# Score blocks of a linear recurrence in a compact tile, masked once for all row groups

## The chip, the cores and the metric

One Trainium2 chip, of which the kernel uses 1 core. The metric is the device time of one execution in microseconds (us), the median of several runs. A core has five engines with a queue of instructions each: TensorE (PE) multiplies matrices, VectorE (DVE) and ScalarE (ACT) work on elements, GpSimd (POOL) does small work, and SyncE (SP) starts transfers. An engine runs its queue in order and waits at an instruction until its operands are there.

## The reference

A decoder trunk of two layers over 256 tokens of width 2048. Each layer projects the normed input with `w_in`, runs sliding-window attention on one half of the heads and a gated linear recurrence (HGRN2) on the other, projects both with `w_out`, and then has a feed-forward block. The change touches the recurrence and the scaling of attention's outputs:

```python
f = lbf + (1.0 - lbf) * jax.nn.sigmoid(z)
k_in = (1.0 - lbf) * jax.nn.sigmoid(-z)
...
b = jnp.cumsum(g_, axis=2)                       # g = log f
decay = jnp.exp(where(causal, b_t - b_s, MASK))  # per channel
a = jnp.einsum('bhtk,bhsk,bhtsk->bhts', q_, k_, decay)
o = jnp.einsum('bhts,bhsv->bhtv', a, v_) + (q_ * exp(b)) @ state
...
o = rms_norm(o, hgrn_gain)
attn = rms_norm(sliding_window_attention(q, k, v, sinks), attn_gain)
```

`a` is a lower triangle of scores whose decay differs from channel to channel.

## The kernel before

Matrix products with weights are made from high and low halves: a weight chunk (`wr`, 128x1024, fetched by SP) is cast by ACT into `wh` (L310), DVE subtracts to get `wl` (L320), and PE makes three products for each tile, xh·wh, xl·wh and xh·wl (L335, L336, L338), twelve matmuls 128x512 a chunk. The input's halves are `ck`.

In a layer, `w_in` is walked in strips of 512 columns: attention's k and v, two strips of q, and then for each of two groups of four recurrence heads the strips f, q, i and g. A group is an object of class `Rec`, whose work runs beside the matmuls of the next strips:

- `done_f` makes f and k with sigmoids and scales f by the bound `lb` (ACT, L951); `done_q` makes q and the pair operand `qd`.
- `levels` computes the triangle of scores by doubling. First PE computes blocks of 32 tokens from `k` and `qd` (`pd`). `up(1)` and `prepare(2)` scale q, k and f for the next step on DVE. Then `four(2, 8)` and `four(8)` (scores L1024, from `qf` of L1010 and L1012) each join four blocks of 2 and of 8 tokens inside the blocks of 32, `up_four` (L1049 to L1059) scales for what comes next, and the loop over 32 and 64 (scores L1097, copies L1101) joins blocks outside them. `up(32)` is the second use of L993.
- The blocks of 32 lie on the diagonal of the 128x128 score tile `at`. They come from PSUM with masks: a product with the identity (L1075), predicated copies with `m_one` (L1077) and three with `m_four` a step (L1039). As the place in `at` differs for each of the four groups of 32 rows, each of them has its own set of instructions, on 32 partitions.
- `out` multiplies `at` with the values `hv` (L1129), `done_i` makes `hv` (L1120), and `px` is the block between both halves of the tokens. The result goes through a transposing store and load (`turn`, `nat`) to `split_shuffled`, which scales with a gain and splits into halves.

A scheduler sets the order of each engine's instructions: it goes by the program's order, in which `yield` and `later(n, ...)` put steps of the recurrence behind parts of the strips, and by `behind(...)`, which puts a step after a named matmul. POOL builds the masks at the start.

Of the kernel before, what the change touches and what calls it, by code (L numbers as in the profile page):

```python
# [8 lines left out]
F32 = mybir.dt.float32  # L9
# [38 lines left out]
def decoder(ctx: ExitStack, tc: tile.TileContext, x, p, positions, w_in, attn_sinks,  # L48
# [126 lines left out]
    def gain_cols(base, l, n):  # L175
        return gT[:, base + l * n: base + (l + 1) * n]
# [99 lines left out]

        return a.rearrange("p k (a j) -> p k a j", a=4)

    def split_shuffled(d, gcols, hl, t, wide=False):
        d, = d  # L280
        h, lo = (quarters(a[:, :, t * P:(t + 1) * P]) for a in hl)
        if gcols is None:
            split(d, h, lo)
            return
        for b in range(4):
            g = gcols[:, b:b + 1]
            if wide:
                S.activation(d[:, b], d[:, b], AF.Copy, scale=g)
            else:
                S.activation(h[:, b], d[:, b], AF.Copy, scale=g)  # L290
                V.scalar_tensor_tensor(lo[:, b], d[:, b], g, h[:, b].bitcast(F32),
                                       op0=ALU.mult, op1=ALU.subtract)
        if wide:
            split(d, h, lo)

    def new_ck():
        return [xp.tile([P, 4, SEQ], F32R, tag="ck", name="ck", bufs=14) for i in range(2)]
# [297 lines left out]
    m_up = cp.tile([P, P], F32, name="m_up")  # L595
    m_prev = cp.tile([P, P], F32, name="m_prev")
    m_neg = cp.tile([P, P], F32, name="m_neg")
    m_one = cp.tile([P, 64], F32, name="m_one")
    m_four = cp.tile([P, 2, 192], F32, name="m_four")
    lb = cp.tile([P, DEPTH, 8], F32, name="lb")  # L600
    omlb = cp.tile([P, DEPTH, 8], F32, name="omlb")
    sink = cp.tile([P, DEPTH, 16], F32, name="sink")
# [5 lines left out]
    def constants():  # L608
# [9 lines left out]
        select(m_prev, ones, [[1, P]], -1, -1)  # L618
        G.memset(m_neg, 0.0)
        select(m_neg, m_neg, [[-1, P]], 0, 1, fill=NEG)  # L620
        select(m_one, ones[:, :64], [[-2, 64]], 0, 1)
        select(m_one, m_one, [[2, 64]], 0, -1)
        for si, k in enumerate((2, 8)):
            m = m_four[:, si].rearrange("p (b six k) -> p b six k", six=6, k=k)
            for v0, n in ((0, 3), (3, 2), (5, 1)):
                for base, sign in ((0, 1), (k - 1, -1)):
                    select(m[:, :, v0:v0 + n], ones[:, :32 * n] if sign > 0 else m[:, :, v0:v0 + n],
                           [[-4 * k * sign, 32 // k], [-k * sign, n], [0, k]], base, sign)

        lmax = tiny(8)  # L630
        V.tensor_copy(lmax, lbl[:, 0])
# [123 lines left out]
    for l in range(DEPTH):  # L755
# [56 lines left out]
        def attend(half, t, o):  # L812
            d = shuffled(o, ready=True)
            for _ in range(6):
                yield
            S.copy(quarters(qT[half][:, :, t * P:(t + 1) * P]), d[0])
            yield
            yield from head_pair(half, t)
            if half == 1:
                yield  # L820
                r = sum_rstd(ssa[t], 1024, f"ra{t}")
                d = []
                for h in range(2):
                    b = nat()
                    V.tensor_scalar(turn_order(b), ao[t][:, h].rearrange("p (k q i) -> p k q i", k=4, q=4),
                                    r[:, 0:1], None, op0=ALU.mult)
                    d.append(b)
                for _ in range(18 + 4 * t):
                    yield
                d = [shuffled(b, ready=True) for b in d]  # L830
                for h in range(2):
                    for _ in range(5 - 4 * h):
                        yield
                    split_shuffled(d[h], gain_cols(96, l, 8)[:, 4 * h:4 * h + 4], attn[h], t,
                                   wide=True)

        def head_pair(half, t):

# [80 lines left out]
        class Rec:  # L919


            def __init__(s, grp):
                s.grp = grp
                s.has_v = set()
                s.f = sp.tile([P, 4, SEQ], F32, tag="A", name="f")
                s.k = sp.tile([P, 4, SEQ], F32, tag="B", name="k")
                s.q = sp.tile([P, 4, SEQ], F32, tag="C", name="q")
                s.at = sp.tile([P, NT, 4, P], F32, tag="at", name="at")
                s.ax = sp.tile([P, 4, P], F32, tag="ax", name="ax")
                G.memset(s.at, 0.0)  # L930

            def diagonal(s, j):

                rows = slice(32 * j, 32 * j + 32)
                return rows, s.at[rows].rearrange("p t h m -> p (t h) m")[:, :, rows]

            def done_f(s, t, ps):
                z = nat()
                S.activation(z, ps, AF.Copy, scale=rx(t)[:, 0:1])


                def turn():
                    pt = bank((P, 4, P))
                    for b in range(4):
                        T.transpose(pt[:, b], z[:, b * P:(b + 1) * P], ident)
                    cols = slice(t * P, (t + 1) * P)
                    S.activation(s.f[:, :, cols], pt, AF.Sigmoid)
                    S.activation(s.k[:, :, cols], pt, AF.Sigmoid, scale=-1.0)
                    for h in range(4):
                        c = s.grp * 4 + h  # L950
                        S.activation(s.f[:, h, cols], s.f[:, h, cols], AF.Identity,  # L951
                                     scale=omlb[:, l, c:c + 1], bias=lb[:, l, c:c + 1])
                later(5, turn)

            def done_q(s, t, ps):
# [56 lines left out]
                V.tensor_tensor(qf[:, :, 5], qf[:, :, 4], fv[:, :, 1].to_broadcast([P, n, k]),  # L1012
                                op=ALU.mult)

            def four(s, k, n=None):

                pl = bank((P, NT, 4, 48))
                for t in range(NT):
                    for h in range(4):
                        for j in range(4):  # L1020
                            rows = slice(32 * j, 32 * j + 32)
                            c = h * 64 + t * 32 + 8 * j
                            with behind("pe"):
                                T.matmul(pl[rows, t, h].rearrange("p (b six k) -> p b six k", six=6, k=k),  # L1024
                                         s.k[:, h, t * P + 32 * j:t * P + 32 * j + 32],
                                         s.qf[:, :, c:c + 8].rearrange("p v (b k) -> p b v k", k=k),
                                         start=True, stop=True)
                s.up_four(k)
                if n:
                    s.prepare(n)  # L1030
                for j in range(4):
                    rows, at = s.diagonal(j)
                    at = at.rearrange("p g (b m) -> p g b m", m=4 * k)
                    pv = pl[rows].rearrange("p t h (b m) -> p (t h) b m", m=6 * k)
                    mv = m_four[rows, (2, 8).index(k), 48 * j:48 * j + 48].rearrange(
                        "p (b m) -> p b m", m=6 * k)
                    for v0, n in ((0, 3), (3, 2), (5, 1)):
                        cols = slice(v0 * k, (v0 + n) * k)
                        V.copy_predicated(  # L1039
                            at[:, :, :, (4 - n) * k:4 * k],  # L1040
                            mv[:, :, cols].bitcast(I32).unsqueeze(1)
                            .to_broadcast([32, 8, 8 // k, n * k]),
                            pv[:, :, :, cols])

            def up_four(s, k):
                qv, kv, fv, qf = s.views(k)
# [14 lines left out]
            def levels(s):  # L1061
# [7 lines left out]
                                     s.qd[:, h, t, j], start=True, stop=True)  # L1069
                s.up(1)  # L1070
                s.prepare(2)
                for j in range(4):
                    rows, at = s.diagonal(j)
                    pv = pd[rows].rearrange("p t h m -> p (t h) m")
                    V.tensor_tensor(at, pv[:, :, 0:32], ident[rows, rows].unsqueeze(1)  # L1075
                                    .to_broadcast([32, 8, 32]), op=ALU.mult)
                    V.copy_predicated(  # L1077
                        at.rearrange("p g (b two) -> p g b two", two=2)[:, :, :, 1],
                        m_one[rows, 16 * j:16 * j + 16].bitcast(I32).unsqueeze(1)
                        .to_broadcast([32, 8, 16]), pv[:, :, 32:48])  # L1080
                yield
                yield
                yield
# [2 lines left out]
                yield  # L1086
                yield
                s.four(8)
                yield
                yield  # L1090
                for k in (32, 64):
# [48 lines left out]
            def done_g(s, t, ps):  # L1140
                sg = nat()
                S.activation(sg, ps, AF.Silu, scale=rx(t)[:, 0:1])
                o = s.ot[:, t].rearrange("p h d -> p (h d)")
                V.tensor_tensor(o, o, sg, op=ALU.mult)
                c = 2 + s.grp
                if c not in mix:
                    mix[c] = new_ck()
                gcols = gain_cols(112, l, 8)[:, 4 * s.grp:4 * s.grp + 4]
                if s.grp == 1:
                    later(4, lambda: split_T(blocks4(o), gcols, mix[c], t))  # L1150
                    return
                d = shuffled(o)
                later(6, lambda: split_shuffled(d, gcols, mix[c], t, wide=True))

        if l == 0:
            with tc.issue_after(first.ins):
# [204 lines left out]
```

## Time and profile before

| | |
|---|---|
| median of 3 runs | 2382.85 us (2382.56 to 2384.52) |
| the profiled execution | 2381.94 us |
| its span, first to last instruction | 2380.2 us |
| granted TensorE clock, mean | 0.998 |
| PE busy | 2343.6 us, 98% of the span |
| DVE, ACT, POOL busy | 2012.1, 1424.4, 115.6 us |
| bytes read and written in HBM | 474.57 and 29.36 MB |

The busy time of PE overlaps its weight loads (PEld). A large matmul's duration is modelled and longer than the distance between two starts. Idle time of PE is what the other engines can add to the end. A row of the waits names the waiting line, the awaited one, the sum, the number and the longest. A row of the groups ends with busy us, mean ns of one, and the idle time ahead of them.

### The profile page before, as it was taken

The page shows a single profiled execution, that of the slowest core. Times are in us where ns is not written, and L with a number is a line of the kernel's source. Part 1 is how long each engine was busy: PE and PEld are TensorE (multiplying, and loading weights), DVE is VectorE, ACT ScalarE, POOL GpSimd, SP SyncE. Part 2 cuts the span into 40 slices and gives each one's busy share as a digit, 9 for nine tenths or more (in the row PEclk, how much of TensorE's full clock was granted, in tenths as well). Part 3 has the DMA queues.
Part 4 walks back from the last instruction along what each step waited for, and adds up shares of the span by engine and source line. Part 5 has one row for each costly group of instructions (what it writes and reads, how often), then busy time and mean ns, then how long its engine had stood idle before and what let it go on. Part 6 is the DMA issues. An engine that isn't in the chain of part 4 may idle for free.

```text
span 2380.2 us, 32807 instructions
## 1 busy us (share of the span) xinstructions
PE 2343.6 (98%) x11527; PEld 1928.1 (81%) x11527; DVE 2012.1 (85%) x2587; ACT 1424.4 (60%) x2072; POOL 115.6 (5%) x217
## 2 busy tenths in 40 slices
PE   9999999999999999999999999999999999999999
PEld 7887787887888888888788777878878888888887
DVE  7676987899999899888877769878999989998885
ACT  6565566556556555657656565665666565565564
POOL 4100001000000000001010000010000000000010
PEclk9999999999999999999999999999999999999999
DMA  8656457656566764766776464675765675667753
GB/s 288 217 160 221 160 196 257 219 199 231 190 230 206 254 225 168 259 228 202 240 217 210 140 226 150 224 269 176 236 224 192 207 254 197 230 208 252 243 169 133
DMA packets 301669, 506.11 MB, mean 213 GB/s; under 512 B 23712, under 2 KB 69696, under 8 KB 301504
## 3 DMA queue, kind: packets, MB, share of 16 engines
q1 hardware_dynamic: 301200, 503.93, 63.1%
q8 instruction: 90, 1.47, 0.3%
q14 instruction: 75, 0.61, 0.1%
q10 hardware_dynamic: 240, 0.07, 0.0%
q0 software_dynamic: 64, 0.02, 0.0%
HBM read 474.57 MB, written 29.36 MB: 212 GB/s over the span
## 4 chain that ended last, share of the span: by engine, by line
PE 87%; DVE 9%; issue 1%; ACT 1%; POOL 1%; DMA 1%; SPq 0%; DVEq 0%; ACTq 0%; POOLq 0%
PE acc L338 8%; PE acc L335 8%; PE acc L336 8%; PE accc L426 5%; PE accc L427 5%; PE accc L423 5%; PE acca L427 4%; PE acca L423 4%; PE acce L427 4%; PE acca L426 4%; PE acce L423 4%; PE acce L426 4%; PE accd L427 3%; PE accd L423 3%; PE accd L426 3%; PE ms L423 3%
## 5 line engine op out<-in xcount | busy, mean ns | idle before, releaser
L310 ACT CAST wh<-wr 128x1024 fp32r<-128x1024 f32 x980 | 1005.3, 1052 | 684.4 <-DVE wr L439 212.2
L320 DVE TENSOR_TENSOR wl<-wr,wh 128x1024 fp32r<-128x1024 f32 x980 | 1162.7, 1220 | 213.9 <-ACT wh L310 206.8
L335 PE MATMUL acc<-wh,ck 128*128 128x512 f32 x1056 | 419.9, 398 | 2.3 <-ACT wh L310 1.8
L338 PE MATMUL acc<-wl,ck 128*128 128x512 f32 x1056 | 412.5, 393 | 4.6 <-DVE wl L320 4.5
L336 PE MATMUL acc<-wh,ck 128*128 128x512 f32 x1056 | 414.7, 393 | 0.0
L439 DVE TENSOR_TENSOR wr<-wr 128x1024 f32<-128x1024 f32 (+1 forms) x240 | 244.5, 1044 | 0.9
L338 PEld LDWEIGHTS acc<-wl,ck 128*128 128x128 f32 x1056 | 199.3, 189 | 49.2 <-DVE wl L320 7.4
L335 PEld LDWEIGHTS acc<-wh,ck 128*128 128x128 f32 x1056 | 199.4, 189 | 44.5 <-ACT wh L310 2.6
L336 PEld LDWEIGHTS acc<-wh,ck 128*128 128x128 f32 x1056 | 199.5, 189 | 40.0 <-DVE ck L204 0.5
L423 PE MATMUL acca<-wh,ck 128*128 128x512 f32 x468 | 183.2, 392 | 3.1 <-ACT wh L310 3.1
L427 PE MATMUL acca<-wl,ck 128*128 128x512 f32 x468 | 182.9, 391 | 1.0 <-DVE wl L320 1.0
L423 PE MATMUL acce<-wh,ck 128*128 128x512 f32 x468 | 183.1, 391 | 0.4 <-ACT wh L310 0.4
L427 PE MATMUL acce<-wl,ck 128*128 128x512 f32 x468 | 182.8, 391 | 0.3 <-DVE wl L320 0.3
L426 PE MATMUL acca<-wh,ck 128*128 128x512 f32 x468 | 182.6, 390 | 0.0
L426 PE MATMUL acce<-wh,ck 128*128 128x512 f32 x468 | 182.5, 390 | 0.0
L427 PE MATMUL accd<-wl,ck 128*128 128x512 f32 x368 | 144.9, 394 | 0.0
L423 PE MATMUL accd<-wh,ck 128*128 128x512 f32 x368 | 143.8, 391 | 0.0
L426 PE MATMUL accd<-wh,ck 128*128 128x512 f32 x368 | 143.4, 390 | 0.0
L426 PE MATMUL accc<-wh,ck 128*128 128x512 f32 x368 | 143.4, 390 | 0.0
L427 PE MATMUL accc<-wl,ck 128*128 128x512 f32 x368 | 143.3, 390 | 0.0
L423 PE MATMUL accc<-wh,ck 128*128 128x512 f32 x368 | 143.3, 389 | 0.0
L423 PEld LDWEIGHTS acca<-wh,ck 128*128 128x128 f32 x468 | 88.1, 188 | 22.9 <-ACT wh L310 4.8
(276 smaller groups left out, 3329.4 us busy)
## 6 DMA issues: line engine op xcount, KB each, us to landing
wr<-in_w_in_dram SPq DMA_DIRECT2D x176, 512.0 KB, 5.1
wr<-in_w_ffn_gate_dram SPq DMA_DIRECT2D x176, 512.0 KB, 5.8
wr<-in_w_ffn_up_dram SPq DMA_DIRECT2D x176, 512.0 KB, 6.1
wr<-in_w_ffn_down_dram SPq DMA_DIRECT2D x176, 512.0 KB, 7.2
wr<-in_w_out_dram SPq DMA_DIRECT2D x64, 512.0 KB, 4.9
wr<-in_w_ple_gate_dram SPq DMA_DIRECT2D x64, 512.0 KB, 5.2
turn<-nat SPq DMA_DIRECT2D x86, 256.0 KB, 2.7
nat<-turn SPq DMA_DIRECT2D x344, 64.0 KB, 3.6
```

The lines of the kernel that those rows point to most:

```text
L310: marks["hi"] = S.copy(hi, raw)
L320: marks["lo"] = V.tensor_tensor(lo, raw, hi.bitcast(F32), op=ALU.subtract)
L335: T.matmul(ps[t], xh, hi[:, k], start=first, stop=False)
L336: T.matmul(ps[t], xl, hi[:, k], start=False, stop=False)
L338: marks[t, c] = marks["pe"] = T.matmul(ps[t], xh, lo[:, k], start=False, stop=last)
L423: T.matmul(ps, xh, hi[:, k], start=id(ps) not in opened, stop=False, skip_group_check=True)
L426: T.matmul(ps, xl, hi[:, k], start=False, stop=False, skip_group_check=True)
L427: marks["pe"] = T.matmul(ps, xh, lo[:, k], start=False, stop=k == ks[-1], skip_group_check=True)
L439: V.tensor_tensor(dst, p, q, op=ALU.subtract)
```

## The change

Four parts:

1. The blocks of 32 tokens of all four row groups go to one compact tile `ac` of 128 partitions x 8 x 32, so each mask operation is one instruction over 128 partitions. Four ACT copies then bring them to the diagonal of `at`. The masks are compact (`m_same`, `m_one`, `m_four`), cut on POOL at the start out of the wide ones.
2. `split_shuffled` loses its `wide` form: attention's outputs and those of group 0 are scaled by ACT straight into the high half, with one DVE scalar_tensor_tensor for each quarter, where ACT scaled in place, cast 128x512, and DVE subtracted once.
3. The scaling of `f` moves from ACT to DVE.
4. The planner's order follows from these.

```diff
-    def split_shuffled(d, gcols, hl, t, wide=False):
+    def split_shuffled(d, gcols, hl, t):
...
-            if wide:
-                S.activation(d[:, b], d[:, b], AF.Copy, scale=g)
-            else:
-                S.activation(h[:, b], d[:, b], AF.Copy, scale=g)
-                V.scalar_tensor_tensor(lo[:, b], d[:, b], g, h[:, b].bitcast(F32),
-                                       op0=ALU.mult, op1=ALU.subtract)
-        if wide:
-            split(d, h, lo)
+            S.activation(h[:, b], d[:, b], AF.Copy, scale=g)
+            V.scalar_tensor_tensor(lo[:, b], d[:, b], g, h[:, b].bitcast(F32),
+                                   op0=ALU.mult, op1=ALU.subtract)
...
+        for j in range(4):
+            rows = slice(32 * j, 32 * j + 32)
+            G.tensor_copy(m_same[rows], ident[rows, rows])
+            G.tensor_copy(m_one[rows], one[rows, 16 * j:16 * j + 16])
+            G.tensor_copy(m_four[rows], four[rows, :, 48 * j:48 * j + 48])
...
+                s.ac = sp.tile([P, NT * 4, 32], F32, tag="ac", name="ac")
...
-                        S.activation(s.f[:, h, cols], s.f[:, h, cols], AF.Identity,
-                                     scale=omlb[:, l, c:c + 1], bias=lb[:, l, c:c + 1])
+                        V.tensor_scalar(s.f[:, h, cols], s.f[:, h, cols], omlb[:, l, c:c + 1],
+                                        lb[:, l, c:c + 1], op0=ALU.mult, op1=ALU.add)
...
-                for j in range(4):
-                    rows, at = s.diagonal(j)
...
-                    for v0, n in ((0, 3), (3, 2), (5, 1)):
-                        cols = slice(v0 * k, (v0 + n) * k)
-                        V.copy_predicated(
...
+                at = s.ac.rearrange("p g (b m) -> p g b m", m=4 * k)
...
+                for v0, n in ((0, 3), (3, 2), (5, 1)):
+                    cols = slice(v0 * k, (v0 + n) * k)
+                    V.copy_predicated(
...
+                pv = pd.rearrange("p t h m -> p (t h) m")
+                V.tensor_tensor(s.ac, pv[:, :, 0:32], m_same.unsqueeze(1)
+                                .to_broadcast([P, 8, 32]), op=ALU.mult)
+                V.copy_predicated(
+                    s.ac.rearrange("p g (b two) -> p g b two", two=2)[:, :, :, 1],
+                    m_one.bitcast(I32).unsqueeze(1).to_broadcast([P, 8, 16]), pv[:, :, 32:48])
...
                 s.four(8)
+                for j in range(4):
+                    rows = slice(32 * j, 32 * j + 32)
+                    S.copy(s.at[rows].rearrange("p t h m -> p (t h) m")[:, :, rows], s.ac[rows])
...
-                later(6, lambda: split_shuffled(d, gcols, mix[c], t, wide=True))
+                later(6, lambda: split_shuffled(d, gcols, mix[c], t))
```

DVE's order at the first score block of group 0 in layer 0. L1077, L1075 and L1039 are the masked operations of one row group each; L1049 to L1057 are `up_four`. Before:

```order
L1077 COPY_PREDICATED at<-m_one,ms 32x8x16
L1075 TENSOR_TENSOR at<-ms,ident 32x8x32
L1049 TENSOR_TENSOR q<-q,f 128x128x2
L1077 COPY_PREDICATED at<-m_one,ms 32x8x16
L1075 TENSOR_TENSOR at<-ms,ident 32x8x32
L1050 TENSOR_TENSOR q<-qf,f 128x128x4
L1077 COPY_PREDICATED at<-m_one,ms 32x8x16
L1055 TENSOR_TENSOR k<-k,f 128x256x2
L1039 COPY_PREDICATED at<-m_four,ms 32x8x4x6
L1056 TENSOR_TENSOR f<-f 128x256
L1039 COPY_PREDICATED at<-m_four,ms 32x8x4x4
L1057 TENSOR_TENSOR k<-k,f 128x128x4
```

The same place after, where line numbers are about five lower (L1034 is the masked copy of a step, L315 the low half of a weight chunk, L1010 the last operation of `qf`):

```order
L1044 TENSOR_TENSOR q<-q,f 128x128x2
L1010 TENSOR_TENSOR qf<-qf,f 128x256
L315 TENSOR_TENSOR wl<-wr,wh 128x1024
L1045 TENSOR_TENSOR q<-qf,f 128x128x4
L1050 TENSOR_TENSOR k<-k,f 128x256x2
L1034 COPY_PREDICATED ac<-m_four,ms 128x32x6
L1051 TENSOR_TENSOR f<-f 128x256
L1034 COPY_PREDICATED ac<-m_four,ms 128x32x4
L1052 TENSOR_TENSOR k<-k,f 128x128x4
L1034 COPY_PREDICATED ac<-m_four,ms 128x32x2
L1054 TENSOR_TENSOR f<-f 128x128
L315 TENSOR_TENSOR wl<-wr,wh 128x1024
```

The masked operations of the row groups are one each, and two weight chunks' low halves stand among the level's operations, where before there was none.

ACT's order where the scores of group 0 are done and the values come (L1120 and L1115 make `hv`, L1101 and L1096 copy the scores of the 32- and 64-steps). Before:

```order
L310 CAST wh<-wr 128x1024
L1120 ACTIVATE hv<-acc_1626,rx_503 128x512
L1120 ACTIVATE hv<-acc_1627,rx_533 128x512
L1101 COPY at<-ms 32x8x32 x2
L1101 COPY at<-ms 64x8x64
L310 CAST wh<-wr 128x1024 x2
```

After, with the copies out of the compact tile in L1083:

```order
L1115 ACTIVATE hv<-acc_1641,rx_517 128x512
L1115 ACTIVATE hv<-acc_1642,rx_547 128x512
L1083 COPY at<-ac 32x8x32 x4
L1096 COPY at<-ms 32x8x32 x2
L305 CAST wh<-wr 128x1024
L1096 COPY at<-ms 64x8x64
L305 CAST wh<-wr 128x1024
```

Four copies stand between `hv` and the copies of the 32-step, and a weight cast comes between those and the copy of the 64-step.

More of the change, by code (lines that the diff above doesn't have):

```diff
@@ L597, in decoder @@
     m_neg = cp.tile([P, P], F32, name="m_neg")
-    m_one = cp.tile([P, 64], F32, name="m_one")
-    m_four = cp.tile([P, 2, 192], F32, name="m_four")
+    m_one = cp.tile([P, 16], F32, name="m_one")
+    m_four = cp.tile([P, 2, 48], F32, name="m_four")
+    m_same = cp.tile([P, 32], F32, name="m_same")
     lb = cp.tile([P, DEPTH, 8], F32, name="lb")
@@ L620, in constants @@
         select(m_neg, m_neg, [[-1, P]], 0, 1, fill=NEG)
-        select(m_one, ones[:, :64], [[-2, 64]], 0, 1)
-        select(m_one, m_one, [[2, 64]], 0, -1)
+        wide = nat((P, 512))
+        one, four = wide[:, 0:64], wide[:, 64:448].rearrange("p (s m) -> p s m", s=2)
+        select(one, ones[:, :64], [[-2, 64]], 0, 1)
+        select(one, one, [[2, 64]], 0, -1)
         for si, k in enumerate((2, 8)):
-            m = m_four[:, si].rearrange("p (b six k) -> p b six k", six=6, k=k)
+            m = four[:, si].rearrange("p (b six k) -> p b six k", six=6, k=k)
             for v0, n in ((0, 3), (3, 2), (5, 1)):
@@ L833, in attend @@
                         yield
-                    split_shuffled(d[h], gain_cols(96, l, 8)[:, 4 * h:4 * h + 4], attn[h], t,
-                                   wide=True)
+                    split_shuffled(d[h], gain_cols(96, l, 8)[:, 4 * h:4 * h + 4], attn[h], t)
         def head_pair(half, t):
@@ L929, in __init__ @@
                 s.ax = sp.tile([P, 4, P], F32, tag="ax", name="ax")
+                s.ac = sp.tile([P, NT * 4, 32], F32, tag="ac", name="ac")
                 G.memset(s.at, 0.0)
-            def diagonal(s, j):
-                rows = slice(32 * j, 32 * j + 32)
-                return rows, s.at[rows].rearrange("p t h m -> p (t h) m")[:, :, rows]
             def done_f(s, t, ps):
@@ L1013, in prepare, with four @@
                                 op=ALU.mult)
-            def four(s, k, n=None):
+            def four(s, k, following=None):
                 pl = bank((P, NT, 4, 48))
@@ L1028, in four @@
                 s.up_four(k)
-                if n:
-                    s.prepare(n)
-                for j in range(4):
-                    rows, at = s.diagonal(j)
[L1033 to L1036, printed above, removed]
-                    for v0, n in ((0, 3), (3, 2), (5, 1)):
-                        cols = slice(v0 * k, (v0 + n) * k)
[L1039 to L1043, printed above, removed]
+                if following:
+                    s.prepare(following)
+                at = s.ac.rearrange("p g (b m) -> p g b m", m=4 * k)
+                pv = pl.rearrange("p t h (b m) -> p (t h) b m", m=6 * k)
+                mv = m_four[:, (2, 8).index(k)].rearrange("p (b m) -> p b m", m=6 * k)
+                for v0, n in ((0, 3), (3, 2), (5, 1)):
+                    cols = slice(v0 * k, (v0 + n) * k)
+                    V.copy_predicated(
+                        at[:, :, :, (4 - n) * k:4 * k],
+                        mv[:, :, cols].bitcast(I32).unsqueeze(1)
+                        .to_broadcast([P, 8, 8 // k, n * k]),
+                        pv[:, :, :, cols])
             def up_four(s, k):
@@ L1071, in levels @@
                 s.prepare(2)
[L1072 to L1080, printed above, removed]
+                pv = pd.rearrange("p t h m -> p (t h) m")
[4 more added lines that the diff above has]
+                    m_one.bitcast(I32).unsqueeze(1).to_broadcast([P, 8, 16]), pv[:, :, 32:48])
                 yield
```

## The prediction

> **What bounds the kernel now.** I read the page first: busy time by engine, then the chain that ended last.
>
> ```profile
> span 2380.2 us, 32807 instructions
> PE 2343.6 (98%) x11527; PEld 1928.1 (81%) x11527; DVE 2012.1 (85%) x2587; ACT 1424.4 (60%) x2072; POOL 115.6 (5%) x217
> PE 87%; DVE 9%; issue 1%; ACT 1%; POOL 1%; DMA 1%; SPq 0%; DVEq 0%; ACTq 0%; POOLq 0%
> ```
>
> TensorE is busy 98% of the span, and the change takes no matmul from it. So the change can win only what PE stands idle, 2380.2 - 2343.6 = 36.6 us over the whole program, and of that only what lies at the places it touches. DVE's 9% of the chain says that its work is what PE waits for. The second view is PE's list of waits (waiting line, awaited line, total us, times, longest):
>
> ```profile
> PE acc L338 <- DVE wl L320: 4.5, 6, 1.0
> PE ms L1097 <- DVE k L993: 4.5, 2, 2.2
> PE ms L1097 <- DVE k L1057: 4.5, 4, 1.2
> PE ms L1024 <- DVE qf L1012: 2.5, 2, 1.3
> ```
>
> These 16.0 us are the waits for operands of the recurrence's levels (k, qf) and for the low halves of weights. Once per layer PE waits 2.2 us for k of L993, once 1.3 for qf, twice up to 1.2 for k of L1057. The third view is the windows: engine busy time in 40-us stretches, for each layer the first score stretch (group 0), the strip between, and the second score stretch (group 1), then some short windows.
>
> ```profile
> core 0: us, PE busy (x) PEld busy (x) DVE busy (x) ACT busy (x) POOL busy (x), PEclk, DMA share, GB/s
> 160.00:200.00 40.00, 35.72 (x387) 27.99 (x385) 37.05 (x72) 18.30 (x29) 1.93 (x1) 1.00 0.37 113
> 215.00:255.00 40.00, 39.04 (x179) 31.79 (x178) 21.01 (x23) 35.35 (x66) 0.00 (x0) 1.00 0.69 231
> 255.00:295.00 40.00, 36.73 (x383) 29.40 (x382) 38.81 (x75) 17.36 (x25) 0.00 (x0) 1.00 0.42 142
> 1340.00:1380.00 40.00, 35.66 (x385) 27.72 (x383) 37.79 (x73) 17.70 (x28) 1.13 (x1) 1.00 0.36 106
> 1397.00:1437.00 40.00, 39.04 (x179) 31.80 (x178) 21.60 (x23) 35.82 (x68) 0.00 (x0) 1.00 0.69 233
> 1437.00:1477.00 40.00, 36.69 (x376) 29.39 (x375) 38.81 (x75) 16.70 (x24) 0.00 (x0) 0.96 0.42 139
> 145.00:158.00 13.00, 13.00 (x84) 11.64 (x83) 8.55 (x15) 10.60 (x25) 2.77 (x8) 1.00 0.41 146
> 287.29:290.70 3.41, 1.84 (x19) 1.68 (x20) 3.27 (x7) 0.58 (x1) 0.00 (x0) 1.00 0.61 207
> 290.70:294.12 3.42, 3.42 (x20) 2.88 (x19) 3.29 (x7) 1.77 (x2) 0.00 (x0) 1.00 0.00 0
> 1468.24:1471.65 3.41, 1.44 (x18) 1.36 (x19) 3.24 (x8) 0.29 (x1) 0.00 (x0) 1.00 0.71 252
> 1471.65:1475.07 3.42, 3.42 (x10) 2.68 (x9) 3.29 (x6) 1.66 (x3) 0.00 (x0) 0.50 0.00 1
> ```
>
> In the score stretches DVE is full (37 to 39 of 40 us) and PE idles 4.28, 3.27, 4.34 and 3.31 us. In the strip between, ACT is the full engine (35.35, 35.82) and DVE half empty, and PE idles 0.96 twice. Together 17.12 us, nearly half of PE's idle time. A gap hides a little more than its idle time, as PE's timeline at the longest wait shows (start, us, instruction, idle before):
>
> ```profile
> 1467.37 0.39 PE L336 MATMUL acc<-wh,ck 128*128 128x512 f32 x1
> 1467.59 0.39 PE L338 MATMUL acc<-wl,ck 128*128 128x512 f32 x1
> 1470.21 1.12 PE L1097 MATMUL ms<-q,k 128*64 128x64 f32 x16 [2.23 <-DVE k L993]
> ```
>
> Large matmuls start about 0.23 us apart but last 0.39, so each gap costs 0.16 more than its idle row. With some four gaps in a group-0 stretch, two in a group-1 stretch and one in the strip, PE loses about 4.9, 3.6 and 1.1 us per layer, 19.2 us in all. That is the whole prize, short of the clock: the window from 1471.65, right behind the one with PE busy for only 1.44 us, was granted 0.50 and held 10 matmuls, at the cost of at most half the window, 1.7 us. The window behind 1.84 busy us (287.29) kept 1.00.
>
> **The change part by part.** *Score masks.* The groups with their durations (busy us, mean ns):
>
> ```profile
> L1039 DVE COPY_PREDICATED at<-m_four,ms 32x192 f32<-32x192 int32 x32 | 13.0, 406 | 0.6
> L1039 DVE COPY_PREDICATED at<-m_four,ms 32x128 f32<-32x128 int32 x32 | 9.4, 293 | 0.7
> L1039 DVE COPY_PREDICATED at<-m_four,ms 32x64 f32<-32x64 int32 x32 | 8.2, 257 | 0.7
> L1077 DVE COPY_PREDICATED at<-m_one,ms 32x128 f32<-32x128 int32 x16 | 7.0, 440 | 0.3
> L1075 DVE TENSOR_TENSOR at<-ms,ident 32x256 f32<-32x256 f32 x16 | 6.7, 418 | 0.2
> L868 DVE COPY_PREDICATED nat<-m_prev,ms 128x512 f32<-128x512 int32 x8 | 5.9, 735 | 0.0
> L320 DVE TENSOR_TENSOR wl<-wr,wh 128x1024 fp32r<-128x1024 f32 x980 | 1162.7, 1220 | 213.9 <-ACT wh L310 206.8 <-PE ms L427 3.3 <-DMA nat<-turn 1.5
> ```
>
> There are four recurrences (two groups, two layers). In each, four of L1075 become one, four of L1077 one, and 24 of L1039 six. The new ones have the same elements per partition on 128 partitions instead of 32. No row has that shape on 128. The bounds: each new copy costs what a 32-row one does, or four times that, and then nothing is won. L868, a predicated copy on 128 partitions, takes 735 ns for 512 elements. The 32-row copies give 406 for 192 and 257 for 64, 1.2 ns an element, so 512 would be about 0.8 us by them. The partitions cost nothing. I take the first bound. Saved per recurrence: 3 x 0.418 + 3 x 0.440 + 6 x (0.406 + 0.293 + 0.257) = 8.3 us of DVE, 33 in all. Starts get closer too:
>
> ```profile
> 172.15 0.43 DVE L1039 COPY_PREDICATED at<-m_four,ms 32x192 f32<-32x192 int32 x1
> 172.46 0.59 DVE L1056 TENSOR_TENSOR f<-f 128x256 f32<-128x256 f32 x1
> 174.34 0.43 DVE L1039 COPY_PREDICATED at<-m_four,ms 32x192 f32<-32x192 int32 x1
> 174.81 0.69 DVE L1010 TENSOR_TENSOR qf<-q,f 128x512 f32<-128x512 f32 x1
> ```
>
> Behind the copy of the first row group the next instruction starts 0.31 us after it and overlaps it; behind the same copy of a later group it starts 0.47 after it. 0.16 us for each of the 24 operations in later groups is about 4 us more per recurrence; I count it as margin. [...]
>
> *What the order puts in their place.* In the first score block the new order has two weight casts (1.22 each) between the level's operations where before there was none, and two attention transposes stand there too. So not all 8.3 us come off what PE waits for. At the qf wait some 2.6 us of the first mask operations and 1 us of later ones are gone, and 2.4 come in: it is the one wait in doubt, and the two k waits behind it have all the saving. The casts that came late before are then early, which is why no new wait for wl stands in their place.
>
> *The copies.* A new step on ACT: four copies 32x256 out of the compact tile, behind the last masked operation and ahead of the copies of L1101 (L1096 in the new numbering); the product of hv and at waits for them.
>
> ```profile
> L1101 ACT COPY at<-ms 32x256 f32<-32x256 f32 x8 | 2.9, 362 | 9.2 <-PE ms L1097 9.1
> L310 ACT CAST wh<-wr 128x1024 fp32r<-128x1024 f32 x980 | 1005.3, 1052 | 684.4 <-DVE wr L439 212.2 <-PE acca L426 178.4 <-PE acc L336 107.6
> L951 ACT ACTIVATE f<-f,lb,omlb 128x128 f32<-128x128 f32 x32 | 13.1, 490 | 0.0
> L291 DVE SCALAR_TENSOR_TENSOR ck<-nat,gT,ck 128x128 fp32r<-128x128 f32 x24 | 6.9, 348 | 0.4 <-ACT ck L290 0.4
> L204 DVE TENSOR_TENSOR ck<-nat,ck 128x512 fp32r<-128x512 f32 x64 | 43.9, 688 | 21.7 <-ACT ck L203 11.5 <-DMA wr<-in_w_in_dram 7.8 <-DMA nat<-turn 2.3
> L203 ACT CAST ck<-nat 128x512 fp32r<-128x512 f32 x64 | 39.4, 618 | 9.4 <-DVE nat L215 6.8 <-DMA nat<-turn 1.8
> ```
>
> Four by 0.36 is 1.45 us per recurrence, while ACT is busy 17 to 18 of 40 us there. A wh cast stands between the copies and the 64-row copy behind them. PE reaches the product after the 64-step's scores, which themselves need DVE's later levels, so I cost the copies at nothing; their cover is the two remaining levels. If it is gone they cost 1.45 plus a cast of 1.05, 2.5 us per recurrence.
>
> *f.* Eight scalings 128x128 per recurrence go from ACT (8 x 0.49 = 3.9 us) to DVE. No row has the form; L291 of the same size but two tensors takes 0.348, so 2.8 us at most. For group 0 they fall about 145 to 158, where DVE is busy 8.55 of 13 us, for group 1 in the strip with 19 idle DVE us of 40. Both hide it.
>
> *Scaled splits.* Six calls per layer: four scalings and a cast 128x512 and a subtraction become four scalings and four L291-like operations. ACT loses 6 x 0.618 = 3.7 us, DVE gets 24 x 0.348 - 6 x 0.688 = 4.2 more, mostly in the strip between. There ACT was full and its wh casts late, which made wl late: the 0.96 us. With 3.9 + 3.7 us off ACT this wait should go.
>
> *Masks at the start.* Twelve small copies on POOL, before anything reads them at about 165 us; POOL is 5% busy. Nothing. SP's queue keeps its order.
>
> *The sum.* Group-1 stretches: DVE needs to be 2.2 and 1.2 us sooner and loses 8.3, so all 3.6 goes, 7.2 in both layers. Group-0 stretches: 4.9, of which I leave 0.9 for the qf wait and PE's changes of operand, so 4.0, 8.0 in both. The strip: 1.0 each, 2.0. Together 17.2. The clock dip should go with its wait (1.7), but other dips may come, and I count none. 2381.94 - 17.2 = 2364.7 against the profiled execution; the median of the runs, 2382.85, is 0.9 above that execution, so about 2366.
>
> **The rivals.** *Half.* The new order's casts and transposes keep the group-0 chain as late as it was; only group 1 and the strip gain: 9.2 us, 2373.7. For it: DVE was 37 of 40 busy and stays the fullest engine there. Against: 8.3 us less, about 4 of casts and transposes added.
>
> *All of it.* The closer starts count as well, the last 0.9 and the dip go: 19.2 + 1.7 = 21, 2362. For it: the overlap in the timeline. Against: PE's own changes of operand in the small matmuls stay.
>
> *Slower: the product waits for ACT.* ACT runs its queue in order, so the four copies stand behind two scalings of hv and casts, and the 64-row copy behind another cast that may wait for a buffer that PE has to free. Then PE's product of hv and at waits, and all weight chunks behind it in PE's order. It takes 4.3 us per recurrence to eat the 17.2 and 5.5 to be slower by more than 0.2%; at 6, 4 x 6 - 17.2 = +6.8, 2389.7. For it: a step that four engines' work now passes one after the other. Against: ACT half idle there, and 2.5 us is the price of the rows.
>
> *No change.* The waits come back under other names because casts move in wherever masks moved out; or 128-partition operations cost four times. Within 0.2% (4.8 us, about what a measurement of this kernel tells from none) of 2382.9. L868 speaks against the second.
>
> **How the numbers follow.** The forecast has 0.53, all of it 0.14, half 0.21, no change 0.07, slower 0.05. Faster: 0.53 + 0.14 + 0.21 = 0.88. The range goes from 2360 (all, with 2 us for dips that fall otherwise) to 2377 (half, with 3 us of the copies' price); by itself the forecast holds from 2363 to 2370.
>
> **What would show it.** Right: the new masked operations at 0.26 to 0.44 us on 128 partitions; PE's waits for k ahead of the 64-step and for wl in the strip gone from the list, PE idle under 1.5 us in the group-0 windows; ACT under 32 of 40 us in the strip. Wrong: a wait of PE's product for at by ACT; the masked operations above 1 us; qf waits of over 1 us as before; or new idle time where the gated outputs are split.

## The result and the profile after

The changed kernel takes 2358.06 us, the median of 4 runs (2356.94 to 2358.96), against 2383.68 us for the kernel before (4 runs, 2382.56 to 2384.83): a ratio of 0.9892, 95% interval 0.9875 to 0.9909. In a second set of runs (experiment 5) it was 2359.77 against 2381.25 us, 0.9912 (0.9898 to 0.9925). Faster was forecast, but by less: 2366, in a range that began at 2360.

The page of the kernel after, top and chain:

```profile
span 2357.0 us, 32796 instructions
PE 2336.2 (99%) x11527; PEld 1925.1 (82%) x11527; DVE 1990.8 (84%) x2559; ACT 1413.9 (60%) x2044; POOL 119.2 (5%) x229
PE 92%; DVE 5%; issue 1%; DMA 1%; POOL 1%; ACT 1%; SPq 0%; DVEq 0%; ACTq 0%; POOLq 0%
```

DVE's share of the chain fell from 9 to 5%. PE's waits after:

```profile
PE acca L418 <- ACT wh L305: 3.4, 4, 1.3
...
PE ms L418 <- ACT nat L427: 2.0, 1, 2.0
...
PE acc L333 <- DVE wl L315: 0.8, 2, 0.4
...
PE ms L1022 <- DVE qf L1010: 0.3, 1, 0.3
```

All waits for k are gone, qf keeps 0.3 us of 2.5, and of the 4.5 for wl 0.8 are left. What stands at the top now lies in other stages. The wait in the strip between the score stretches is another one than the prediction took it for. PE waited there for ACT's cast `wh` itself, 0.9 us a layer, and not for `wl`, whose waits lay in the group-0 stretches (1.8 us a layer). Its row in the list of before, which is gone after the change:

```profile
PE acc L335 <- ACT wh L310: 1.8, 2, 0.9
```

The windows of the two layers' score stretches and of the strip between, in the order of the prediction:

```profile
core 0: us, PE busy (x) PEld busy (x) DVE busy (x) ACT busy (x) POOL busy (x), PEclk, DMA share, GB/s
160.00:200.00 40.00, 39.90 (x408) 32.38 (x407) 34.61 (x60) 20.95 (x30) 2.99 (x3) 1.00 0.55 165
215.00:255.00 40.00, 40.00 (x245) 32.98 (x244) 30.51 (x52) 27.66 (x44) 0.00 (x0) 1.00 0.71 240
255.00:295.00 40.00, 40.00 (x352) 32.98 (x351) 32.85 (x50) 21.09 (x29) 2.01 (x2) 1.00 0.38 119
1340.00:1380.00 40.00, 39.70 (x290) 32.85 (x289) 30.19 (x48) 20.36 (x27) 2.98 (x3) 1.00 0.55 167
1397.00:1437.00 40.00, 40.00 (x305) 32.83 (x304) 32.09 (x52) 24.56 (x34) 0.00 (x0) 1.00 0.61 201
1437.00:1477.00 40.00, 40.00 (x294) 33.16 (x293) 33.24 (x45) 23.91 (x35) 2.01 (x2) 1.00 0.43 138
```

PE idles 0.40 us in all six, where it idled 17.12. (The program runs ahead of its old times by up to 23 us, so the later windows don't hold quite the same work.) The groups of new operations:

```profile
L949 DVE TENSOR_SCALAR f<-f,omlb,lb 128x128 f32<-128x128 f32 x32 | 8.9, 342 | 11.8 <-ACT f L945 11.8
L1034 DVE COPY_PREDICATED ac<-m_four,ms 128x192 f32<-128x192 int32 x8 | 3.2, 404 | 0.0
L1034 DVE COPY_PREDICATED ac<-m_four,ms 128x128 f32<-128x128 int32 x8 | 2.3, 293 | 0.0
L1034 DVE COPY_PREDICATED ac<-m_four,ms 128x64 f32<-128x64 int32 x8 | 2.1, 262 | 0.0
L1070 DVE COPY_PREDICATED ac<-m_one,ms 128x128 f32<-128x128 int32 x4 | 1.8, 445 | 0.0
L1068 DVE TENSOR_TENSOR ac<-ms,m_same 128x256 f32<-128x256 f32 x4 | 1.7, 418 | 0.0
L1083 ACT COPY at<-ac 32x256 f32<-32x256 f32 x16 | 6.4, 402 | 0.2
```

A masked operation over 128 partitions takes what one over 32 took: 404, 293, 262, 445, 418 ns against 406, 293, 257, 440, 418.

Where the 23.2 us between the two spans came from shows when one sets the start of the same weight cast (the n-th of 1000 on ACT, from the timelines) in both traces side by side:

| cast | place | before, us | after, us | ahead |
|---|---|---|---|---|
| 11th | start-up | 33.64 | 31.52 | 2.1 |
| 41st | before the first scores | 122.72 | 120.56 | 2.2 |
| 141st | behind layer 0's scores | 417.43 | 405.29 | 12.1 |
| 221st | feed-forward, layer 0 | 581.11 | 567.64 | 13.5 |
| 541st | layer 1, before its scores | 1303.88 | 1292.03 | 11.9 |
| 621st | behind layer 1's scores | 1542.84 | 1519.67 | 23.2 |

The two layers' score stretches and strips give 10.0 and 11.3 us; 1.7 of the latter is the clock dip at 1471.65 (an estimate: half of 3.41 us at a granted 0.50), so 19.6 are waits. A dip of before at 550 went (+1.3) and one of after at 1144.67 came (-1.6). The 2.1 us of the start-up are not a fixed part of the change; experiment 1 takes them up.

### The profile page after: what moved, and what is told of

The parts are those of the page before. It is cut to its first block, busy times and chain, and to the rows that moved or that the text cites. A ratio compares the mean times of both kernels' runs of the same rounds, so it can differ in the third digit from the quotient of the medians.

```text
span 2357.0 us, 32796 instructions
## 1 busy us (share of the span) xinstructions
PE 2336.2 (99%) x11527; PEld 1925.1 (82%) x11527; DVE 1990.8 (84%) x2559; ACT 1413.9 (60%) x2044; POOL 119.2 (5%) x229
## 4 chain that ended last, share of the span: by engine, by line
PE 92%; DVE 5%; issue 1%; DMA 1%; POOL 1%; ACT 1%; SPq 0%; DVEq 0%; ACTq 0%; POOLq 0%
PE acc L330 9%; PE acc L331 9%; PE acc L333 9%; PE accc L421 5%; PE accc L422 5%; PE accc L418 5%; PE acca L422 4%; PE acce L422 4%; PE acca L421 4%; PE acca L418 4%; PE acce L418 4%; PE acce L421 4%; PE accd L422 3%; PE accd L421 3%; PE accd L418 3%; PE ms L418 3%
## 5 line engine op out<-in xcount | busy, mean ns | idle before, releaser
L315 DVE TENSOR_TENSOR wl<-wr,wh 128x1024 fp32r<-128x1024 f32 x980 | 1163.7, 1219 | 232.2 <-ACT wh L305 223.3
L418 PEld LDWEIGHTS acca<-wh,ck 128*128 128x128 f32 x468 | 87.9, 188 | 23.2 <-ACT wh L305 5.1
```

What stands on the lines that cost most here:

```text
L315: marks["lo"] = V.tensor_tensor(lo, raw, hi.bitcast(F32), op=ALU.subtract)
L418: T.matmul(ps, xh, hi[:, k], start=id(ps) not in opened, stop=False, skip_group_check=True)
```

## The experiments

The kernel before is run beside each. "Held starts" are in the expectations the later starts beside operations of a later row group: 0.47 us behind such an operation, against 0.31 behind one of the first group.

**1. The kernel before again.** 

> The kernel before, unchanged, to see what one profile has in its start-up and its clock dips by chance. In the profile before, TensorE's records give the full clock from 14.2 us on; after the change from 8.0 us on, and the first ten weight chunks came 2.1 us sooner. If that is chance of the clock's phase, this run's time is within 0.1% of the kernel before, its waits in the score stretches are the same 16 us, but the moment of the full clock lies somewhere else and the time of the tenth weight cast (33.6 us) moves with it, by up to 2 us or so. If the start-up gain belongs to the change, the tenth cast stays at 33.6 us here.

Ratio 1.0004 (0.9994 to 1.0015). TensorE's records give the full clock from 6.1 us here (14.2 in the first profile, 8.0 after the change), a half-clock window follows at 9.5, and the 11th cast (the expectation's tenth) starts at 33.2 us, 0.45 sooner than in the first profile. That alone settles little. Over the thirteen profiles of this study the full clock began anywhere from 4.9 to 14.2 us, six times with a half-clock window right behind. In the five where it came by 8.3 us and stayed, the 11th cast starts at 31.3 to 31.6 us; in the other eight it starts at 32.7 to 34.2, the changed kernel's second profile (33.55) among them. So the start-up goes with the moment of the clock, and the changed kernel doesn't always have the 2.1 us. But all five early ones are among the seven kernels with compact masks, and none among the six without. That the change makes the early start more frequent isn't excluded. This profile has four half-clock windows between 180 and 1480 us, where the first one had two; one of them and the window ahead of it:

```profile
286.02:289.44 3.42, 1.18 (x13) 0.78 (x12) 3.21 (x9) 0.00 (x0) 0.00 (x0) 1.00 0.75 249
289.44:292.85 3.41, 3.41 (x16) 2.81 (x14) 3.29 (x6) 1.08 (x2) 0.00 (x0) 0.50 0.14 53
```

It lies where the wait for k of L993 ends: the waits stay in place, but whether a dip follows differs from run to run.

**2. The score blocks alone.** The changed kernel with the splits and f of before.

```diff
-                        V.tensor_scalar(s.f[:, h, cols], s.f[:, h, cols], omlb[:, l, c:c + 1],
-                                        lb[:, l, c:c + 1], op0=ALU.mult, op1=ALU.add)
+                        S.activation(s.f[:, h, cols], s.f[:, h, cols], AF.Identity,
+                                     scale=omlb[:, l, c:c + 1], bias=lb[:, l, c:c + 1])
...
-                later(6, lambda: split_shuffled(d, gcols, mix[c], t))
+                later(6, lambda: split_shuffled(d, gcols, mix[c], t, wide=True))
```

> Only the compact score blocks, their masks and the four copies; splits and f as before. Theory one (the masked operations by row group are what made the level operands and wl late): all waits for qf and k go, 9 to 10 us per layer less the strip's 1.1, so 16 to 18 us faster, ratio about 0.993, and the wait for wl in the strip between (about 1.0 us idle) stays. Rival (ACT's relief by f and splits does a good part): under 12 us, with waits for wl left in the score stretches. Second rival (the four copies need the freed ACT): PE waits for at by ACT, visible as idle time ahead of the product with hv.

2357.72 us, ratio 0.9903 (0.9888 to 0.9918): the whole gain, more than either theory gave. PE was busy 40.00 of 40 us in all six windows; the strip's wait, which was to stay, went too.

**3. The splits and f alone.** The kernel before with those two parts.

> Only the scaled splits and f on DVE; score blocks by row group as before. Theory one: the strip's wait goes (2 us over both layers) and nothing else, or DVE's extra operations make the score stretches worse by up to 2 us: between 2 us faster and 2 us slower, ratio 0.999 to 1.001, and the waits for qf and k as long as before. Rival: 6 us or more faster.

2380.15 us, 0.9996 (0.9987 to 1.0005). The strip's wait went, as expected, but the score stretches' waits grew, and one for `at` of 0.7 us a layer is new:

```profile
PE ms L1091 <- DVE k L987: 7.4, 2, 3.7
PE ms L1018 <- DVE qf L1006: 3.8, 2, 2.0
PE ms L1091 <- DVE k L1051: 3.5, 3, 1.7
```

14.7 us for k and qf instead of 11.5: what PE gained in the strip it gave back at the next level, whose operands come no sooner.

**4. Row groups into the compact tile.** Here and below, lines that only change their indentation stand as unchanged.

```diff
+                for j in range(4):
+                    R = slice(32 * j, 32 * j + 32)
                     for v0, n in ((0, 3), (3, 2), (5, 1)):
...
-                            at[:, :, :, (4 - n) * k:4 * k],
+                            at[R, :, :, (4 - n) * k:4 * k],
```

(and so for the product and `m_one`.)

> The changed kernel, but each masked operation again once per row group, 32 partitions at a time, into the compact tile; copies, splits and f as changed. Theory one: the DVE time comes back, 8.3 us and the held starts per recurrence, and with it the waits: within 4 us of the kernel before, on top of that the strip's wait gone; if the copies on ACT cost anything, slower than the kernel before. Rival (the compact tile and the changed order carry the gain, not the number of operations): at most 8 us slower than the changed kernel.

2380.02 us, 0.9997 (0.9988 to 1.0006). The compact tile, its copies, the splits and f are all there, and nothing is won; against experiment 3, which has no copies, nothing is lost by them either. The gain hangs on the masked operations by row group. Two things differ there: how many they are, and where they start.

**5. The changed kernel again**, beside the next three.

> The changed kernel, unchanged, on the same chip and beside the same runs as the next three. The score blocks alone gave a ratio of 0.9903. Theory one (splits and f add nothing): the same here within 0.15%, 0.989 to 0.992. Theory two, on the clock: TensorE's waits in the score stretches bring windows of half clock behind them; without the waits the mean granted clock stands at 0.998 to 0.999 in every run, where the kernel before has 0.995 to 0.999, and that is 3 to 5 us of the gain over the 19 us of waits.

2359.77 us, 0.9912 (0.9898 to 0.9925), not told apart from the score blocks alone. The mean granted clock was 0.998 or 0.999 in its 4 runs, 0.9988 on the mean, and 0.9972 on the mean of the 36 runs of the kernel before beside experiments 1 to 8 (0.995 to 0.999). 0.0016 to 0.0018 of 2380 us is about 4 us.

**6. Four times over all partitions.**

```diff
+                for j in range(4):
                     V.tensor_tensor(s.ac, pv[:, :, 0:32], m_same.unsqueeze(1)
                                     .to_broadcast([P, 8, 32]), op=ALU.mult)
...
```

(and so for the joining copies)

> The changed kernel with each masked operation given four times over all 128 partitions, which writes the same values: as many masked operations as before, 32 per recurrence, of the same duration, but none starts in another group of 32 partitions. If the number of operations is all that counts (8.3 us of DVE per recurrence), it stands where the row-group version stood, 2378 to 2382 us, with the same waits. If the held starts count too (0.16 us at some 24 to 36 places per recurrence, about 4 us), the waits for k shrink by up to 4 us a recurrence and it is 6 to 16 us faster than the row-group version, 2364 to 2374.

2356.01 us, 0.9899 (0.9884 to 0.9914): as fast as the changed kernel, with four times its masked operations, and below what both expectations gave. Two of their groups and the first window, in which DVE is as full as before and PE without a pause:

```profile
L1035 DVE COPY_PREDICATED ac<-m_four,ms 128x192 f32<-128x192 int32 x32 | 12.8, 400 | 0.0
L1072 DVE COPY_PREDICATED ac<-m_one,ms 128x128 f32<-128x128 int32 x16 | 7.0, 441 | 0.0
```

```profile
160.00:200.00 40.00, 40.00 (x408) 32.53 (x408) 36.25 (x75) 20.82 (x28) 1.02 (x1) 1.00 0.54 172
```

So fewer operations aren't needed. But the repeats, which write one and the same tile, stand later in DVE's order here, and nine low halves of weights stand among them in place of four. That left the order as a rival to the starts, and asked for the ninth run.

**7. Two halves of 64 partitions.** As 4, with `range(2)` and `R = slice(64 * j, 64 * j + 64)`.

> The changed kernel with each masked operation in two halves of 64 partitions: 16 masked operations per recurrence, two thirds of the saving (5.5 us of 8.3 and most of the held starts). The waits at a recurrence were 3.6 to 4.9 us, so if they are simply DVE's lateness, the saving still covers the group-1 waits and most of group 0: 2358 to 2364 us. If the gain is in proportion to the operations, a third of it is lost: 2364 to 2368.

2362.34 us, 0.9923 (0.9911 to 0.9936), inside the first expectation. In group 0 the first wait of the chain is back, with two smaller ones at L1096 (0.9 and 0.6 us over both layers):

```profile
PE ms L1022 <- DVE qf L1010: 2.5, 2, 1.4
```

**8. The copies three times.**

```diff
+                    for _ in range(3):
                         S.copy(s.at[rows].rearrange("p t h m -> p (t h) m")[:, :, rows], s.ac[rows])
```

> The changed kernel with each of the four ACT copies out of the compact tile given three times: 8 x 0.40 = 3.2 us more of ACT per recurrence ahead of the copies that PE's product waits for. If two levels of DVE and PE work cover them as forecast (price nothing), the time stays within 0.1% of the changed kernel. If the copies stand close to the path, PE waits for at ahead of the product of hv and at, up to 3 us per recurrence, 4 to 12 us slower in all.

2361.15 us, 0.9918 (0.9905 to 0.9932), against 0.9912 beside it: not told apart by the time. The trace tells more; in group 0 PE's product waits for ACT:

```profile
PE ms L1125 <- ACT at L1097: 1.9, 2, 1.0
```

The eight copies added, 8 x 0.40 = 3.2 us a recurrence, reach the path by 1.0 us in group 0 and not in group 1. So the cover of the four copies there is about 2.2 us.

**9. The kernel before, each masked operation over all partitions.** No compact tile, no copies, splits and f as before. The wide masks are zero in the other rows, so an operation may run over all of them.

```diff
-                return rows, s.at[rows].rearrange("p t h m -> p (t h) m")[:, :, rows]
+                return rows, s.at.rearrange("p t h m -> p (t h) m")[:, :, rows]
...
-                    pv = pl[rows].rearrange("p t h (b m) -> p (t h) b m", m=6 * k)
-                    mv = m_four[rows, (2, 8).index(k), 48 * j:48 * j + 48].rearrange(
+                    pv = pl.rearrange("p t h (b m) -> p (t h) b m", m=6 * k)
+                    mv = m_four[:, (2, 8).index(k), 48 * j:48 * j + 48].rearrange(
...
-                    V.tensor_tensor(at, pv[:, :, 0:32], ident[rows, rows].unsqueeze(1)
+                    V.tensor_tensor(at, pv[:, :, 0:32], ident[:, rows].unsqueeze(1)
...
-                        m_one[rows, 16 * j:16 * j + 16].bitcast(I32).unsqueeze(1)
+                        m_one[:, 16 * j:16 * j + 16].bitcast(I32).unsqueeze(1)
```

> The kernel before, with its 32 masked operations per recurrence, in its order but for single weight casts, without a compact tile, copies, splits or f of the change. Only each masked operation runs over all 128 partitions (with the wide masks, whose other rows are zero, so the values are the same). If held starts are what the row groups cost, the operations keep their 0.26 to 0.44 us and DVE's busy sum stays at some 2012 us, but starts overlap as they do among operations of one group, and the waits for qf and k fall below a third: 15 to 23 us faster than the kernel before, ratio 0.990 to 0.994. If the order of the changed program made room (weight casts among the levels, masked operations given behind the chain because of the shared tile), nothing changes here: ratio 0.999 to 1.001, 16 us of waits.

2360.04 us, 0.9914 (0.9901 to 0.9928). DVE's order is that of before but for two weight operations a layer that move by a place or two. The same two places as in the prediction, in its timeline:

```profile
170.50 0.43 DVE L1039 COPY_PREDICATED at<-m_four,ms 128x192 f32<-128x192 int32 x1
170.79 0.62 DVE L1056 TENSOR_TENSOR f<-f 128x256 f32<-128x256 f32 x1
...
172.58 0.43 DVE L1039 COPY_PREDICATED at<-m_four,ms 128x192 f32<-128x192 int32 x1
172.88 0.66 DVE L1010 TENSOR_TENSOR qf<-q,f 128x512 f32<-128x512 f32 x1
```

Both copies take the 0.43 us that they took, and both times the next instruction starts 0.3 us after, where it was 0.31 and 0.47. The second copy itself starts 0.32 us after the operation ahead of it (172.26), where it was 0.44 (174.34 after 173.90). The start of group 0's masked operations and of what follows their end, before:

```profile
165.14 0.40 DVE L1075 TENSOR_TENSOR at<-ms,ident 32x256 f32<-32x256 f32 x1
...
193.30 2.36 DVE L320 TENSOR_TENSOR wl<-wr,wh 128x1024 fp32r<-128x1024 f32 x2
```

and here:

```profile
165.01 0.41 DVE L1075 TENSOR_TENSOR at<-ms,ident 128x256 f32<-128x256 f32 x1
...
187.33 2.35 DVE L320 TENSOR_TENSOR wl<-wr,wh 128x1024 fp32r<-128x1024 f32 x2
```

28.2 us became 22.3 (group 1: 32.5 became 26.9), with as many masked operations and the same four low halves of weights between (seven in group 1, both times). The waits for k and qf are gone from the list. What is left in these stretches is the strip's wait, where ACT is still full, and 0.6 us ahead of a product of `at` and `hv` in layer 0, for which the profile names no releaser:

```profile
PE acc L335 <- ACT wh L310: 1.8, 2, 0.9
...
PE ms L1129 <- issue: 0.6, 1, 0.6
```

```profile
160.00:200.00 40.00, 39.42 (x406) 31.80 (x406) 37.37 (x78) 21.60 (x32) 3.95 (x3) 1.00 0.49 160
215.00:255.00 40.00, 39.04 (x238) 31.55 (x237) 23.83 (x29) 33.84 (x63) 0.00 (x0) 1.00 0.72 248
```

My expectation that DVE's busy sum would stay at 2012 us was wrong: it is 1994.3. Where instructions overlap, the sum counts the shared time once, and it stands below their added durations: the 980 of L320 here, of 1.216 us each, add up to 1192 us and have 1161.5 busy.

**10. The same with the splits and f of the change**, both edits as the diff at the top shows them.

> As the version before with all partitions, with the change's scaled splits and f on DVE as well; still 32 masked operations and no compact tile. That version kept the strip's wait (PE 39.04 of 40 us busy in both strips). If ACT's load makes it, as forecast, the relief takes it away: PE idle under 0.3 us there, 2 us faster than that version, 2357 to 2359 us, and the score stretches stay without waits. If not, the wait stays and the time stays at 2360.

2357.75 us, 0.9902 (0.9889 to 0.9916). The strip is without a pause:

```profile
215.00:255.00 40.00, 40.00 (x246) 33.01 (x245) 29.66 (x56) 28.43 (x49) 0.00 (x0) 1.00 0.74 253
```

This has 32 masked operations per recurrence and no compact tile, and is where the changed kernel is.

**11. Only the joining copies over all partitions**: of the ninth's edit the lines with `pl` and `m_four`, not those with `ident` and `m_one`.

> The kernel before, with only the 24 joining copies per recurrence (m_four) over all partitions; the first eight masked operations (product and m_one) stay by row group, as do f and splits. Three quarters of the held operations are gone. If each held start costs the same, some 4.3 of the 5.7 us per recurrence come back: the waits for k go, a part of the one for qf (1.3 us in group 0) stays, 2361 to 2366 us. If the first block alone were enough to hold the chain, half or more of the 16 us of waits stay: over 2369.

2366.12 us, 0.9936 (0.9923 to 0.9949), 0.1 us above the first expectation's upper end. Group 0's masked stretch takes 23.8 us by the timeline, 4.4 less than before, for 18 of the 24 operations in later row groups; all 24 gave 5.8. That is 0.24 us for each, both times. A part of the first wait stays, and 0.7 us a layer for `wl`:

```profile
PE ms L1024 <- DVE qf L1012: 1.4, 2, 0.7
```

The kernels 2, 5, 6 and 10 all lie at 0.990 to 0.991 with overlapping intervals; none beats the changed one by more than can be told.

## Why the prediction was wrong in size

The waits were the right ones. Two terms of the sum failed: it took 2.4 us too few from the waits, and it put the clock at nothing, which was worth about 4.

*Right.* The place (score stretches and the strip), the waits that go, the price of the operations over 128 partitions (the first bound), the free copies (4, and cover to spare in 8), POOL's masks, and the strip's cause, a full ACT: 9 and 10 show that with the level waits gone its relief alone removes the 2 us. The operand there was misread, `wl` for `wh`, which changes no term. That it went in 2 without this relief was not forecast; 2 also has the new order, and which part of that did it stays open.

*The term on group 0.* I left 0.9 us per layer there for qf and for PE's changes of operand. No run shows what such a change costs PE by itself; in the timelines the first small matmul starts 0.32 us behind a large one (168.53 and 168.85 before), where two large ones are 0.23 apart, and 0.32 after the change as well (166.82 and 167.14). PE idles 0.10 and 0.30 us. Waits brought 19.6 us by the table of casts, where the sum had 17.2 and the whole prize was put at 19.2. The sum was 2.4 us too small. Some 1.4 of it are this term, 1.8 left for both layers against 0.40 found idle; the rest lies in rounding the strip and in the prize itself, and no run separates these.

*The clock, counted as none.* "Other dips may come" weighed a dip that goes against one that comes. The kernel before has more of them than its first profile showed (1), and the kernels without the waits fewer: 0.9972 against 0.9988 on the mean, which as time is an estimate of about 4 us. The forecast had nothing for it, and the range's lower end had 2 us beyond the one dip. This is the largest part of the miss. From 2381, the median of the 36 runs of the kernel before, the estimate then stands at 2381 - 19.6 - 4 = 2357. The profiles agree: in the score stretches the four with the full waits (before, 1, 3, 4) have 1, 3, 4 and 3 half-clock windows; the nine others, with waits of at most 1.4 us there or none, have none. Dips outside these stretches stay, like the one after the change at 1144.67, behind a wait of another stage.

*The profiled execution.* Working from one execution took its start-up and its dips for the kernel's, and the 2382.85 us that the forecast was set from, the median of three runs, stand 1.9 above the 2381 of the 36. The kernel before ranges from 2376.9 to 2386.9 us in the experiments' runs, so the last microseconds of a range had to be wider than the terms of the waits made it.

*The mechanism.* The sum's main term was the number of masked operations, 8.3 us of DVE per recurrence; the closer starts were "margin", 4 us. The runs show that the margin was enough: the starts alone, with the number as before, remove the level waits (9, 10). They are worth 5.8 us of DVE time per recurrence in group 0 (5.6 in group 1), and 0.24 us per operation, not the 0.16 that one pair of rows gave: the operation itself starts later, too, behind the one ahead of it (0.44 us, and 0.32 in 9). In 9, where every masked operation starts in the first group of partitions, the 0.47 behind it becomes 0.30 as well. What in DVE makes these starts late no run shows. Whether the number alone would have done it wasn't tried, since fewer operations by row group can't be had with the same work.

The gain has a ceiling, so a second saving on top buys nothing: PE lost 3.6 to 4.9 us per recurrence, and the 5.8 us of the starts already cover that. Nothing is left for the 8.3 of the number to win.

## What to carry to other kernels

Look at the start-to-start distances on DVE, not only at durations: here work split by row groups of 32 partitions cost its neighbours and itself their overlap (0.24 us for each operation in a later group), and one instruction over all partitions with a mask that is zero elsewhere took the same time as one over 32 (404 and 406 ns for 192 elements). The prize is read from the bounding engine's waits, and a saving beyond it buys nothing; a relief upstream (the strip) may come back as a longer wait at the next late operand (14.7 us for k and qf in 3, 11.5 before). And where half-clock windows stand behind waits, as here (3.41 us at 0.50 behind a wait of 2.23), count the dips over many runs' mean clock, not in one profile.

## What the runs showed of the hardware

- A masked DVE operation over 128 partitions cost what it did over 32 (404 and 406 ns for 192 elements); one in a later row group than its neighbours cost 0.24 us of lost overlap (5.8 us for 24 in experiment 9, 4.4 for 18 in 11).
- The half clock came for a window of 3.41 us behind one in which PE was busy for 1.18 us (experiment 1) or 1.44 (before), with no idle time of PE over 2.3 us ahead of it, and it stayed away behind 1.84 (before). In another stage it came behind 1.90 (before, at 550), so the busy time alone doesn't decide.
- The moment of the first full clock ran from 4.9 to 14.2 us over thirteen profiles, and the start of the 11th weight cast, which goes with it, from 31.3 to 34.2 us.
